# Attention of a diffusion step on one core: P left unnormalised, a fixed order in pairs, small value bands

## The chip, the cores and the metric

The kernel runs on one core of a Trainium2 chip. Its engines are TensorE (PE, with its weight loads shown apart as PEld), VectorE (DVE), ScalarE (ACT), GpSimd (POOL) and SyncE (SP, which here only issues DMAs). The metric is the device time of one execution in microseconds. Each engine runs its own instructions in order and waits at semaphores for the others.

## The reference

One step of a two-layer network: layer 0 (even) has one input projection into a recurrence branch and an attention branch and then an output projection, layer 1 (odd) is a gated recurrence. What the change touches is the attention branch of layer 0: 8 heads of 64, 1024 latent tokens on a grid of 16 rows by 64 columns, 128 context tokens.

```python
def row_block(args):                       # one grid row r, all heads
    r, q_r = args
    rs = jnp.clip(r - kh // 2, 0, rows - kh)
    k_blk = lax.dynamic_slice_in_dim(k_grid, rs, kh, axis=2)[:, :, :, col_idx]
    v_blk = lax.dynamic_slice_in_dim(v_grid, rs, kh, axis=2)[:, :, :, col_idx]
    ...
    s_loc = jnp.einsum('bhjqd,bhkjnd->bhjqkn', qb, k_blk).astype(jnp.float32) * scale + bias
    s_loc = jnp.where(valid, s_loc, NEG_INF)
    s_ctx = jnp.einsum('bhjqd,bhcd->bhjqc', qb, k_ctx).astype(jnp.float32) * scale
    s = jnp.concatenate([s_loc..., s_ctx], axis=-1)
    p = jax.nn.softmax(s, axis=-1).astype(v.dtype)
    o = (einsum(p_loc, v_blk) + einsum(p[..., n_loc:], v_ctx))
...
y = jnp.concatenate([o_a * jax.nn.silu(g_a), merge_heads(o_b) * jax.nn.silu(g_b)], axis=-1)
return y @ w_out, ...
```

Each latent query sees a window of 8 rows by 16 columns and all context keys; context queries see context keys only. The output of attention is multiplied by a SiLU gate and projected.

## The kernel before

Everything is float32 to the outside. For the projections each weight tile and each activation is split into a high part (`wh`, `hTh`) and a rest (`wl`, `hTl`), and a product is three matmuls (`mm_f`, L313 to L318). A unit (`unit_f`) is one weight tile of 128 output columns by one of three chunks of 384 tokens: 24 matmuls. A weight tile is loaded by SP (`wraw`, 512 KB), rounded by ACT (`wh`, L77) and subtracted by POOL (`wl`, L186, in `do_split`).

The order of the work is mostly that of the program: a scheduler places the instructions on each engine in advance, within the room that pools of buffers leave. "minis" are 72 tiles of [128, 384], "slabs" 20 tiles of [128, 1160]; PSUM has 3 banks of `ps_mm`, 2 of `ps_a`, 2 of `ps_b`, 1 of `ps_o`. A DMA's issue on SP waits until its target buffer is free, and what stands behind it on SP waits too.

The attention branch works on four pairs of heads, p = 0 to 3. First come the projections: for each pair three weight tiles (keys, queries, gate) of three chunks. The gate's SiLU lands in `yT` (`gate_evac`). Then come 36 items: for each pair eight grid items (half `hf` 0 or 1 of the rows, column block `j` 0 to 3; 128 queries, 384 window keys and 128 context keys, two heads `e`) and one context item. An item has three steps:

- `a_score`: for each head two matmuls into PSUM (L845 window, L848 context; queries are scaled by -1/8, so scores stand negated), the minimum of the context part (L851), one custom DVE instruction that adds the negated, masked bias and takes the minimum on (L852), the exponential on ACT with its sum (L77, `P`), the reciprocal (L856) and the scaling of P (L857).
- `a_trans`: eight 128 x 128 transposes on PE (L882) and two copies out of PSUM on ACT (`PT`, L77).
- `a_pv`: 16 value products (L897) out of the value bands, summed over keys in one bank for the four items of a half; after the fourth the gate in `yT` is multiplied by it (L905; L912 for a context item).

The loop runs transposes two items behind the scores and value products three behind, and the scheduler mixes them. The table `nbm` (mask minus bias, L822) is made by POOL for 42 of 48 tiles and by DVE for 6, each from a bias load `bT` of 192 KB. The value bands are written to DRAM and read back by column block: `band_load`, 16 loads of 256 KB into eight slabs, placed among the projections of pairs 0 to 2. Masks (`mkt`), cached context keys and values (`kc`, `vc`) and the biases of pair 0 are loaded after the first chunk of the last gate; the biases of the next pair at the end of each pair. After attention comes the out projection (L994 to L996), for which three of its eight weights are split during attention's items, the subtraction on DVE.

Of the kernel before, what the change touches and what calls it, by code (L numbers as in the profile page):

```python
# [33 lines left out]
def trunk_kernel(ctx: ExitStack, tc: tile.TileContext, x, wm0, wm, bmr, wfe, wv, woe, wfo, woo, rgw, sm, st0,  # L34
# [277 lines left out]
    def mm_f(o, i, c, k):  # L312
# [3 lines left out]
        PE.matmul(o, w1, hh, start=(k == 0), stop=False)  # L316
        PE.matmul(o, w1, hl, start=False, stop=False)  # L317
        PE.matmul(o, w2, hh, start=False, stop=(k == 7))  # L318

    def unit_f(i, c, tag=None):  # L320
# [4 lines left out]
        for k in range(8):  # L325
            mm_f(o, i, c, k)
# [479 lines left out]
    def mask_load():  # L806
        for v in range(6):
# [27 lines left out]
    def a_score(i):  # L835
        p, hf, j = items[i]
        P = slab("P", (128, 2, 512))
        nm = const.tile([128, 8], F32, name="nm", bufs=3)
        if hf >= 0:
            S = [psum("mm"), psum("o" if i % 2 else "mm")]  # L840
            for e in range(2):
                o0 = 128 + hf * 512 + j * 128
                lq = aq[p][64 * e:64 * e + 64, o0:o0 + 128]
                rk = grid(ak[p], e)[:, 4 * hf:4 * hf + 12, BS[j]:BS[j] + 32]
                PE.matmul(S[e][:, 0:384], lq, rk, start=True, stop=True)  # L845
            for e in range(2):
                o0 = 128 + hf * 512 + j * 128
                PE.matmul(S[e][:, 384:512], aq[p][64 * e:64 * e + 64, o0:o0 + 128],  # L848
                          kc_t[p][64 * e:64 * e + 64, :], start=True, stop=True)
# [523 lines left out]
```

## Time and profile before

| | |
|---|---|
| median of 3 runs | 1288.13 us (1283.86 to 1288.23) |
| profiled execution | 1288.07 us, of which the span is 1286.1 us |
| PE busy | 1207.2 us, 94% of the span |
| DVE, ACT, POOL busy | 685.7, 540.1, 381.2 us |
| projections of the attention branch end | 635.2 us after the span's start |
| attention's value products end | 777.7 us |

Busy time is what an engine's instructions cover; a busy PE may still run at half its clock, which the granted clock shows (1.00 is 2.4 GHz, 0.50 is 1.2 GHz). What follows "[" in a row of a timeline is the engine's idle time before it and what ended it. A DMA share is the mean over the core's 16 DMA engines.

### The profile page before, as it was taken

The numbers are of one execution on the slowest core, as the hardware profiler recorded it, in microseconds if no ns is written. First come the engines' busy times: TensorE is split into PE (matmuls) and PEld (weight loads), VectorE is DVE, ScalarE is ACT, GpSimd is POOL, SyncE is SP. The second block draws the span as 40 slices with busy tenths as digits, with TensorE's granted clock in tenths as the row PEclk, the third lists the DMA queues.
The fourth block names the chain that finished last, engine by engine and source line by source line (L and its number), as shares of the span: only waits on it lengthen the run. The fifth ranks groups of instructions, "written<-read, shape, count | busy, mean of one in ns | idle before, by whom it ended". The sixth has DMA issues, their size and how long they took to land.

```text
span 1286.1 us, 19174 instructions
## 1 busy us (share of the span) xinstructions
PE 1207.2 (94%) x7536; PEld 1083.1 (84%) x7536; DVE 685.7 (53%) x1422; ACT 540.1 (42%) x1065; POOL 381.2 (30%) x271
## 2 busy tenths in 40 slices
PE   4999998999999999998999999999989899988997
PEld 3889998999999997887866667888988789987886
DVE  5547128315455200000267896644678978799844
ACT  3435134324342211111246774314467576676311
POOL 0143032420515110201250420117355564644000
PEclk8999999999998999998969999999989999999999
DMA  9410100111011455523320325223001101112432
GB/s 355 186 34 21 34 17 26 40 48 37 22 35 36 156 172 189 205 87 108 128 99 17 100 83 181 81 98 131 17 26 42 42 25 42 41 33 95 137 129 82
DMA packets 41909, 110.45 MB, mean 86 GB/s; under 512 B 4180, under 2 KB 14804, under 8 KB 41820
## 3 DMA queue, kind: packets, MB, share of 16 engines
q1 hardware_dynamic: 41820, 109.24, 25.2%
q8 instruction: 59, 0.97, 0.3%
q14 instruction: 30, 0.25, 0.1%
HBM read 96.61 MB, written 12.61 MB: 85 GB/s over the span
## 4 chain that ended last, share of the span: by engine, by line
PE 52%; DVE 14%; ACT 6%; issue 4%; DMA 4%; POOL 2%; SPq 1%; POOLq 0%; ACTq 0%; DVEq 0%
PE ps_mm L316 7%; PE ps_mm L318 7%; PE ps_mm L317 7%; PE ps_mm L995 5%; PE ps_mm L996 5%; PE ps_mm L994 5%; DMA wraw<-in_wfe_dram 3%; DVE yT L1137 2%; DVE xc L1061 2%; DVE P L857 2%; ACT P L77 1%; PE ps_a L221 1%; PE ps_mm L339 1%; PE ps_mm L341 1%; PE ps_mm L340 1%
## 5 line engine op out<-in xcount | busy, mean ns | idle before, releaser
L316 PE MATMUL ps_mm<-hTh,wh 128*128 128x384 f32 x936 | 321.2, 347 | 14.6 <-ACT xp L77 4.8
L317 PE MATMUL ps_mm<-hTl,wh 128*128 128x384 f32 x936 | 320.3, 343 | 2.3 <-DVE hTl L307 1.7
L318 PE MATMUL ps_mm<-hTh,wl 128*128 128x384 f32 x936 | 319.8, 342 | 1.1 <-POOL wl L186 1.1
L186 POOL TENSOR_TENSOR wl<-wraw,wh 128x1024 fp32r<-128x1024 f32 x50 | 127.5, 2552 | 284.3 <-ACT wh L77 254.6
L316 PEld LDWEIGHTS ps_mm<-hTh,wh 128*128 128x128 f32 x936 | 178.1, 191 | 31.1 <-ACT kq L77 7.4
L317 PEld LDWEIGHTS ps_mm<-hTl,wh 128*128 128x128 f32 x936 | 178.8, 191 | 4.6 <-DVE hTl L307 3.3
L318 PEld LDWEIGHTS ps_mm<-hTh,wl 128*128 128x128 f32 x936 | 178.7, 191 | 1.9 <-POOL wl L186 1.7
L995 PE MATMUL ps_mm<-wl,yh 128*128 128x512 f32 (+1 forms) x288 | 113.6, 395 | 4.6 <-DVE wl L186 4.6
L996 PE MATMUL ps_mm<-wh,yl 128*128 128x512 f32 (+1 forms) x288 | 112.6, 391 | 0.0
L994 PE MATMUL ps_mm<-wh,yh 128*128 128x512 f32 (+1 forms) x288 | 112.4, 392 | 0.0
L77 ACT ACTIVATE wh<-wraw 128x1024 fp32r<-128x1024 f32 x68 | 71.3, 1058 | 70.5 <-DMA wraw<-in_wfe_dram 40.6
L262 POOL TENSOR_TENSOR ss<-ss,nhalf 128x1 f32<-128x1 f32 x27 | 15.2, 564 | 243.4 <-DVE ss L261 186.2
L339 PE MATMUL ps_mm<-wh,hTh 128*128 128x256 f32 x288 | 83.2, 289 | 2.1 <-ACT va L77 2.1
L341 PE MATMUL ps_mm<-wh,hTl 128*128 128x256 f32 x288 | 82.0, 285 | 0.0
L340 PE MATMUL ps_mm<-wl,hTh 128*128 128x256 f32 x288 | 81.7, 284 | 0.0
L77 ACT ACTIVATE res<-xt 128x512 f32<-128x512 f32 (+1 forms) x37 | 23.0, 621 | 123.6 <-DVE xt L1004 115.7
L995 PEld LDWEIGHTS ps_mm<-wl,yh 128*128 128x128 f32 x288 | 54.5, 189 | 19.4 <-DVE wl L186 7.7
L822 POOL TENSOR_TENSOR nbm<-mkt,bT 128x384 f32<-128x384 f32 x42 | 45.5, 1103 | 85.2 <-DVE nm L868 40.4
L365 DVE SCALAR_TENSOR_TENSOR yT<-yT,ps_mm 128x384 f32<-128x384 f32 x10 | 5.5, 554 | 113.6 <-ACT yT L77 113.6
L994 PEld LDWEIGHTS ps_mm<-wh,yh 128*128 128x128 f32 x288 | 54.4, 189 | 12.3 <-issue 0.3
L996 PEld LDWEIGHTS ps_mm<-wh,yl 128*128 128x128 f32 x288 | 54.6, 189 | 11.4
L1128 POOL TENSOR_TENSOR yT<-yT,rt 128x384 f32<-128x384 f32 x42 | 56.4, 1371 | 23.4 <-ACT rt L77 19.3
(260 smaller groups left out, 2501.1 us busy)
## 6 DMA issues: line engine op xcount, KB each, us to landing
wm<-in_wm_dram SPq DMA_DIRECT2D x48, 512.0 KB
wraw<-in_wfe_dram SPq DMA_DIRECT2D x28, 512.0 KB
xt<-in_x_dram SPq DMA_DIRECT2D x18, 512.0 KB
bT<-in_bias_dram SPq DMA_DIRECT2D x48, 192.0 KB
wraw<-in_wfo_dram SPq DMA_DIRECT2D x16, 512.0 KB
x_d<-xt SPq DMA_DIRECT2D x9, 512.0 KB
xt<-x_d SPq DMA_DIRECT2D x9, 512.0 KB
out_dram<-xt SPq DMA_DIRECT2D x18, 256.0 KB
```

What stands on the lines that cost most here:

```text
L77: i = A.activation(out, in_, func, **kw)
L186: (lo_eng or G).tensor_tensor(lo, r, hi.bitcast(F32), OP.subtract)
L316: PE.matmul(o, w1, hh, start=(k == 0), stop=False)
L317: PE.matmul(o, w1, hl, start=False, stop=False)
L318: PE.matmul(o, w2, hh, start=False, stop=(k == 7))
L339: PE.matmul(o, hh, w1, start=(k == 0), stop=False)
L340: PE.matmul(o, hh, w2, start=False, stop=False)
L341: PE.matmul(o, hl, w1, start=False, stop=(k == 7))
L994: PE.matmul(o[:, :q - p], yh[:, z], wh[:, p:q], start=(k == 0), stop=False)
L995: PE.matmul(o[:, :q - p], yh[:, z], wl[:, p:q], start=False, stop=False)
L996: PE.matmul(o[:, :q - p], yl[:, z], wh[:, p:q], start=False, stop=(k == 7))
L1128: G.tensor_tensor(us[c], us[c], r[:, c * CW:(c + 1) * CW], OP.mult)
```

## The change

1. P is left unnormalised. The sums of a pair's half, [128, 8], are doubled and inverted on DVE (`a_sums`), widened by POOL to [128, 512] (`rbw`), transposed by PE into a `ps_b` bank and multiplied into the gate (`a_gate`). L856 and L857 go. The transposed copy of the second head of every other item goes from ACT to DVE.
2. The instructions of PE and of ACT in attention are chained in program order (`ordered`), and items go in pairs: transposes, scores and value products of two items in a fixed interleaving, the gate's transposes ahead of the value products. The context item of pair 3 comes before its grid items.
3. A band is loaded for a pair of heads: 64 loads of 64 KB into six minis a pair, rather than 16 of 256 KB. The table subtraction is made in place, in the bias's buffer.
4. The projections of pair 3 go by chunk (all three weights at once), with the scores of the first two items after the last chunk's first two units. Weights of pairs 1 and 2 are loaded two ahead. Masks, caches, biases and bands of pair 0 are loaded after the chunks; the rest spread over the items. Four of the out projection's weights are split at items 11, 20, 29 and 32, on POOL.

```diff
+    def ordered(i, eng="PE"):
+
+        if eng in line:
+            after(i.ins, [line[eng]])
+        line[eng] = i.ins.name
         return i
...
-    def band_load(Rg):
-        v0 = vb_d[2 * Rg]
-        for jp in range(2):
-            t = slab("vband", (128, 2, 512))
-            vband[Rg, jp] = t
-            for jj in range(2):
-                load(t[:, jj, :], bass.AP(tensor=v0.tensor, offset=v0.offset + BS[2 * jp + jj] * 512,
-                                          ap=[[64 * 512, 4], [512, 32], [1, 512]]))
+    def band_load(p):
+
+        ts = [mini("vband") for _ in range(6)]
+        for b in range(16):
+            v0 = vb_d[2 * (b // 4)]
+            load(ts[b // 3][:, (b % 3) * 128:(b % 3 + 1) * 128],
+                 bass.AP(tensor=v0.tensor, offset=v0.offset + BS[b % 4] * 512 + p * 128,
+                         ap=[[64 * 512, 4], [512, 32], [1, 128]]))
+            vband[p, b] = ts[b // 3][:, (b % 3) * 128:(b % 3 + 1) * 128]
...
-    def bias_load(p):
-        for hf in range(2):
-            for j in range(3):
-                for h in (2 * p, 2 * p + 1):
-                    t = mini("bT")
-                    s0 = 4 if hf == 0 else 0
-                    ap = bass.AP(tensor=bias.tensor, offset=bias.offset + h * 35328 + j * 736 + s0 * 32,
-                                 ap=[[32, 8], [2208, 16], [1, 384]])
-                    load(t, ap)
-                    n = mini("nbm")
-                    (V if p == 0 and h else G).tensor_tensor(n, mkt[hf * 3 + j], t, OP.subtract)
-                    nbm[h, hf, j] = n
+    def bias_load(p, hf, j):
+        for h in (2 * p, 2 * p + 1):
+            t = mini("bT")
+            s0 = 4 if hf == 0 else 0
+            ap = bass.AP(tensor=bias.tensor, offset=bias.offset + h * 35328 + j * 736 + s0 * 32,
+                         ap=[[32, 8], [2208, 16], [1, 384]])
+            load(t, ap)
+            (V if p == 0 and h else G).tensor_tensor(t, mkt[hf * 3 + j], t, OP.subtract)
+            nbm[h, hf, j] = t
...
+    def a_sums(p, hf):
+
+        sm_ = aSum.pop((p, hf))
+        V.tensor_scalar(sm_, sm_, 2.0, None, OP.mult)
+        V.reciprocal(sm_, sm_)
+        nt = sm_.shape[1]
+        wide = slab("rbw", (128, nt * 128))
+        G.tensor_copy(wide.rearrange("p (j d) -> p j d", d=64),
+                      sm_.rearrange("p j e -> p (j e)")[:, :, None].to_broadcast([128, 2 * nt, 64]))
+        aW[p, hf] = wide
+
+    def a_gate(p, hf):
+
+        wide = aW.pop((p, hf))
+        nt = wide.shape[1] // 128
+        rb = psum("b")
+        for j in range(nt):
+            ordered(PE.transpose(rb[:, j * 128:(j + 1) * 128], wide[:, j * 128:(j + 1) * 128], ident))
+        if hf < 0:
+            yv = yT[4 + p, 0][:, 0:128]
+            V.tensor_tensor(yv, rb[:, 0:128], yv, OP.mult)
+            return
+        rb4 = rb.rearrange("p (j r c) -> p j r c", j=4, r=8)
+        for c, o0, r, n in pieces_of(hf):
+            yv = yT[4 + p, c][:, o0:o0 + n * 64].rearrange("p (r j c) -> p j r c", r=n, j=4)
+            V.tensor_tensor(yv, rb4[:, :, 8 - r % 8 - n:8 - r % 8, :][:, :, ::-1], yv, OP.mult)
...
-                act(P[:, e, :], S[e], AF.Exp, scale=-1.0, bias=nm[:, 4 * e + 1:4 * e + 2],
-                             accum_out=nm[:, 4 * e + 2:4 * e + 3])
-                V.reciprocal(nm[:, 4 * e + 3:4 * e + 4], nm[:, 4 * e + 2:4 * e + 3])
-                V.tensor_scalar(P[:, e, :], P[:, e, :], nm[:, 4 * e + 3:4 * e + 4], 0.5, OP.mult, OP.mult)
...
+    def a_exp(i):
+        p, hf, j = items[i]
+        S, nm = aS.pop(i)
+        P = slab("P", (128, 2, 512))
+        if j == 0:
+            aSum[p, hf] = const.tile([128, 4 if hf >= 0 else 1, 2], F32, name="asum" if hf >= 0 else "asumc", bufs=2)
+        n = 512 if hf >= 0 else 128
+        for e in range(2):
+            ordered(act(P[:, e, 0:n], S[e][:, 0:n], AF.Exp, scale=-1.0, bias=nm[:, 2 * e + 1:2 * e + 2],
+                        accum_out=aSum[p, hf][:, j, e:e + 1]), "ACT")
         aP[i] = P
+        if hf < 0 or j == 3:
+            a_sums(p, hf)
...
+            if e and i % 2:
+                V.tensor_copy(PT[:, e, :n * 128], pt[:, :n * 128])
+            else:
+                ordered(act(PT[:, e, :n * 128], pt[:, :n * 128], AF.Copy), "ACT")
...
-            w_get(i, 0, 1 if i + 1 < IWE else 0)
+            w_get(i, 0 if p == 0 else 2, 1)
...
+    i0 = IP + 9
+    ak[3], aq[3] = slab("kq"), slab("kq")
+    w_split(i0 + 2)
+    for c in range(3):
+        for n in range(3):
+            o = unit_f(i0 + n, c, ("a", "b", "b")[n] if c == 2 else None, ordered if c == 2 else lambda m: m)
+            proj_evac(3, n, c, o)
+            if c == 2 and n < 2:
+                a_score(n)
+                a_exp(n)
+        if c == 0:
+            mask_load(0)
+            kc_load((0,))
+            for j in range(3):
+                bias_load(0, 0, j)
+            band_load(0)
+        elif c == 1:
+            mask_load(1)
+            vc_load()
+            for j in range(3):
+                bias_load(0, 1, j)
+            kc_load((1, 2, 3))
...
     n_it = len(items)
-    for i in range(n_it + 3):
-        if 0 <= i - 2 < n_it:
-            a_trans(i - 2)
-        if i < n_it:
-            a_score(i)
-            p, hf, j = items[i]
-            if hf == 1 and j == 3 and p < 3:
-                bias_load(p + 1)
-            if hf < 0 and p >= 1:
-                w_split(IWE + p - 1, V)
-        if 0 <= i - 3 < n_it:
-            a_pv(i - 3)
+    TB = {(0, 1): (0, 0), (0, 3): (0, 1), (1, 0): (0, 2), (1, 1): (1, 0), (1, 3): (1, 1), (-1, 0): (1, 2)}
+
+    def tables(i):
+
+        p, hf, j = items[i]
+        if p < 3 and (hf, j) in TB:
+            bias_load(p + 1, *TB[hf, j])
+        if p < 3 and hf == 1 and j == 2:
+            band_load(p + 1)
+        if i in WA:
+            w_split(IWE + WA.index(i))
+
+    WA = (11, 20, 29, 32)
+    for m in range(n_it // 2 + 2):
+        ia, ib = 2 * m, 2 * m + 1
+        if 0 <= ia - 2 < n_it:
+            a_trans(ia - 2)
+        if 0 < m and ia < n_it:
+            a_score(ia)
+            a_exp(ia)
+            a_score(ib)
+        if 0 <= ib - 2 < n_it:
+            a_trans(ib - 2)
+        if 0 < m and ia < n_it:
+            a_exp(ib)
+        for i in (ia - 2, ib - 2):
+            if 0 <= i < n_it and (items[i][1] < 0 or items[i][2] == 3):
+                a_gate(*items[i][:2])
+        for i in (ia - 3, ia - 2):
+            if 0 <= i < n_it:
+                a_pv(i)
+        for i in (ia, ib):
+            if i < n_it:
+                tables(i)
     vband.clear()
 
 
```

What moves on POOL, from the last split of the projections' weights to the end of attention's tables: before, all subtractions (`nbm<-mkt,bT`) in one piece, ahead of the next layer's norm (`ss`).

```order
L186 TENSOR_TENSOR wl<-wraw,wh 128x1024
L638 TENSOR_TENSOR oss<-oss,nhalf 128x3 x2
L186 TENSOR_TENSOR wl<-wraw,wh 128x1024 x10
L822 TENSOR_TENSOR nbm<-mkt,bT 128x384 x42
L262 TENSOR_TENSOR ss<-ss,nhalf 128x1 x4
```

In the kernel after, after the same ten splits (`rbw<-asum` is the widening copy of one half of a pair, `asumc` that of a context item; the halves come in order, pair 0 first):

```order
L831 TENSOR_TENSOR bT<-mkt,bT 128x384 x14
L853 COPY rbw<-asum 128x512
L831 TENSOR_TENSOR bT<-mkt,bT 128x384 x12
L853 COPY rbw<-asum 128x512
L853 COPY rbw<-asumc 128x128
L831 TENSOR_TENSOR bT<-mkt,bT 128x384 x6
L195 TENSOR_TENSOR wl<-wraw,wh 128x1024
L831 TENSOR_TENSOR bT<-mkt,bT 128x384 x5
L853 COPY rbw<-asum 128x512
L831 TENSOR_TENSOR bT<-mkt,bT 128x384 x5
L853 COPY rbw<-asum 128x512
```

The copy of the first half of pair 0 stands behind 14 subtractions, that of its second half behind 26, that of the first half of pair 1 behind 37, that of its second half behind all 42.

SP, before, from the band loads among the projections to the biases:

```order
L56 DMA vband<-vb_d 128x1x512 x4
L56 DMA wraw<-in_wfe_dram 128x1024
L56 DMA vband<-vb_d 128x1x512 x4
L59 DMA out_dram<-kq 128x128
L56 DMA wraw<-in_wfe_dram 128x1024
L56 DMA mkt<-in_msk_dram 128x384 x6
L56 DMA kc<-in_kct_dram 128x128 x4
L56 DMA vc<-in_vcd_dram 128x256 x2
L56 DMA bT<-in_bias_dram 128x1x384 x27
L56 DMA wraw<-in_woe_dram 128x1024
L56 DMA bT<-in_bias_dram 128x1x384 x13
```

SP, after, from the loads behind the second chunk of pair 3 on (the row before these is the 16 band loads of pair 0):

```order
L56 DMA mkt<-in_msk_dram 128x384 x3
L56 DMA vc<-in_vcd_dram 128x256 x2
L56 DMA bT<-in_bias_dram 128x1x384 x6
L56 DMA kc<-in_kct_dram 128x128 x3
L56 DMA bT<-in_bias_dram 128x1x384 x8
L56 DMA vband<-vb_d 128x1x128 x16
L56 DMA bT<-in_bias_dram 128x1x384 x12
L56 DMA vband<-vb_d 128x1x128 x16
L56 DMA bT<-in_bias_dram 128x1x384 x5
L56 DMA wraw<-in_woe_dram 128x1024
L56 DMA bT<-in_bias_dram 128x1x384 x7
L56 DMA vband<-vb_d 128x1x128 x16
```

The bands now come as 16 small loads for each pair, between the biases.

PE around the gate of the second half of pair 0 in the kernel after (`P_5823` is the last item of that half, `PT_5810` and `PT_5877` its second and third, `ps_mm_5891` the context item's scores, `ps_mm_5906` the first of pair 1):

```order
L896 MATMUL ps_mm_5891<-kq_4293,kq_4384 128x128
L896 MATMUL ps_mm_5892<-kq_4293,kq_4384 128x128
L886 MATMUL ps_mm_5906<-kq_4615,kq_4729 128x384
L886 MATMUL ps_o_5907<-kq_4615,kq_4729 128x384
L888 MATMUL ps_mm_5906<-kc_5488,kq_4729 128x128
L888 MATMUL ps_o_5907<-kc_5488,kq_4729 128x128
L923 MATMUL ps_a_5917<-cs_71,P_5823 128x128 x4
L923 MATMUL ps_a_5923<-cs_71,P_5823 128x128 x4
L863 MATMUL ps_b_5933<-cs_71,rbw_5828 128x128 x4
L941 MATMUL ps_b_5840<-PT_5810,vband_5358 64x128 x2
L941 MATMUL ps_b_5840<-PT_5810,vband_5360 64x128 x2
L941 MATMUL ps_b_5840<-PT_5810,vband_5361 64x128 x2
```

PE, before, around the same context item's scores (`ps_mm_5917`):

```order
L882 MATMUL ps_a_5780<-cs_71,P_5708 128x128 x4
L897 MATMUL ps_b_5686<-PT_5734,vc_5480 64x128
L845 MATMUL ps_mm_5829<-kq_4293,kq_4384 128x384
L848 MATMUL ps_mm_5829<-kc_5472,kq_4384 128x128
L882 MATMUL ps_a_5815<-cs_71,P_5747 128x128 x4
L861 MATMUL ps_mm_5917<-kq_4293,kq_4384 128x128
L845 MATMUL ps_o_5830<-kq_4293,kq_4384 128x384
L848 MATMUL ps_o_5830<-kc_5472,kq_4384 128x128
L861 MATMUL ps_mm_5918<-kq_4293,kq_4384 128x128
L882 MATMUL ps_a_5821<-cs_71,P_5747 128x128 x4
L897 MATMUL ps_b_5893<-PT_5773,vband_5150 64x128 x2
L897 MATMUL ps_b_5893<-PT_5773,vband_5244 64x128 x2
```

Before, transposes, scores and value products are mixed as the scheduler put them. After, the transposes of the widened sums (L863) stand ahead of the value products in one fixed line.

## Rows read from the trace of the kernel before

**Rows 1.** The page: busy time, share of the span, instructions.

```profile
PE 1207.2 (94%) x7536; PEld 1083.1 (84%) x7536; DVE 685.7 (53%) x1422; ACT 540.1 (42%) x1065; POOL 381.2 (30%) x271
```

**Rows 2.** Timeline, SP’s DMA issues: start, us, line, transfer, count.

```profile
572.07 11.19 SPq L56 DMA_DIRECT2D vband<-vb_d  x4
583.35 2.57 SPq L56 DMA_DIRECT2D wraw<-in_wfe_dram  x1
```

**Rows 3.** Timeline of ACT, same stretch; in brackets its idle time before.

```profile
584.38 1.06 ACT L77 ACTIVATE wh<-wraw 128x1024 fp32r<-128x1024 f32 x1 [10.24 <-issue]
...
596.72 1.06 ACT L77 ACTIVATE wh<-wraw 128x1024 fp32r<-128x1024 f32 x1 [10.52 <-DMA wraw<-in_wfe_dram]
```

**Rows 4.** Timeline of PE around its longest idle time in the projections.

```profile
594.00 0.34 PE L317 MATMUL ps_mm<-hTl,wh 128*128 128x384 f32 x1
594.18 0.34 PE L318 MATMUL ps_mm<-hTh,wl 128*128 128x384 f32 x1
598.80 0.69 PE L316 MATMUL ps_mm<-hTh,wh 128*128 128x384 f32 x1 [4.28 <-DVE yT L365]
...
600.25 0.52 PE L317 MATMUL ps_mm<-hTl,wh 128*128 128x384 f32 x1
600.57 0.52 PE L318 MATMUL ps_mm<-hTh,wl 128*128 128x384 f32 x1
```

**Rows 5.** Windows: busy us (instructions) by engine, granted clock, DMA share, GB/s.

```profile
575.00:600.00 25.00, 18.62 (x101) 17.66 (x100) 1.57 (x3) 4.02 (x7) 5.33 (x3) 0.95 0.28 97
600.00:605.00 5.00, 5.00 (x19) 5.00 (x18) 0.00 (x0) 0.00 (x0) 0.24 (x1) 0.55 0.16 51
...
642.00:662.00 20.00, 19.85 (x74) 11.63 (x76) 11.38 (x31) 8.12 (x21) 15.54 (x15) 0.50 0.41 148
...
740.00:760.00 20.00, 18.24 (x174) 12.63 (x173) 18.14 (x60) 14.09 (x38) 9.30 (x8) 1.00 0.23 73
```

**Rows 6.** Timeline of PE: last projection matmul, first out projections, last value product.

```profile
634.99 0.34 PE L318 MATMUL ps_b<-hTh,wl 128*128 128x384 f32 x1
...
772.07 0.50 PE L994 MATMUL ps_mm<-wh,yh 128*128 128x512 f32 x1
...
777.34 0.48 PE L910 MATMUL ps_b<-PT,vbc 128*64 128x128 f32 x3
```

**Rows 7.** Timeline of PE in a packed stretch: value products, transposes, scores of one item.

```profile
692.87 0.88 PE L897 MATMUL ps_b<-PT,vband 128*64 128x128 f32 x12
...
693.89 1.09 PE L882 MATMUL ps_a<-cs,P 128*128 128x128 f32 x8
694.91 0.92 PE L845 MATMUL ps_mm<-kq 64*128 64x384 f32 x4
...
695.98 0.88 PE L897 MATMUL ps_b<-PT,vband 128*64 128x128 f32 x12
```

**Rows 8.** Groups by line and shape, 635 to 780 us: count, busy us, mean ns.

```profile
L822 POOL TENSOR_TENSOR nbm<-mkt,bT 128x384 f32<-128x384 f32 x41 | 44.5, 1105 | 72.8 <-DVE nm L868 40.4 <-DMA bT<-in_bias_dram 25.8 <-PE ps_mm L848 2.5
...
L857 DVE TENSOR_SCALAR P<-P,nm 128x512 f32<-128x512 f32 x64 | 36.5, 575 | 1.1
...
L856 DVE RECIPROCAL nm<-nm 128x1 f32<-128x1 f32 x64 | 10.1, 160 | 12.5 <-ACT P L77 12.1
...
L905 DVE TENSOR_TENSOR yT<-ps_b,yT 128x256 f32<-128x256 f32 x8 | 3.3, 410 | 0.0
```

**Rows 9.** Windows of one kind of transfer each; columns as in rows 5.

```profile
566.00:571.00 5.00, 5.00 (x31) 5.00 (x30) 0.00 (x0) 0.00 (x0) 0.00 (x0) 1.00 0.26 103
...
625.00:627.00 2.00, 2.00 (x13) 2.00 (x12) 0.00 (x0) 0.00 (x0) 0.00 (x0) 1.00 0.96 286
627.00:628.50 1.50, 1.50 (x11) 1.50 (x10) 0.56 (x1) 0.49 (x1) 0.00 (x0) 1.00 0.45 140
...
710.00:722.00 12.00, 11.50 (x98) 7.80 (x96) 11.37 (x33) 7.38 (x20) 11.45 (x11) 1.00 0.54 172
```

**Rows 10.** Timeline of SP: the first bias issues.

```profile
629.04 3.43 SPq L56 DMA_DIRECT2D bT<-in_bias_dram  x5
```

**Rows 11.** Timeline of POOL: its first subtraction.

```profile
632.92 1.02 POOL L822 TENSOR_TENSOR nbm<-mkt,bT 128x384 f32<-128x384 f32 x1 [12.44 <-DMA bT<-in_bias_dram]
```

More of the change, by code (lines that the diff above doesn't have):

```diff
@@ L80, in act @@
             chain["users"].append(i.ins.name)
+        return i
+    line = {}
+    def ordered(i, eng="PE"):
+        if eng in line:
+            after(i.ins, [line[eng]])
+        line[eng] = i.ins.name
         return i
@@ L315, in mm_f, with unit_f @@
         w1, w2 = wh[:, k * 128:(k + 1) * 128], wl[:, k * 128:(k + 1) * 128]
[L316 to L320, printed above, removed]
+        keep(PE.matmul(o, w1, hh, start=(k == 0), stop=False))
+        keep(PE.matmul(o, w1, hl, start=False, stop=False))
+        keep(PE.matmul(o, w2, hh, start=False, stop=(k == 7)))
+    def unit_f(i, c, tag=None, keep=lambda m: m):
         ucount[0] += 1
@@ L794, in trunk_kernel, with kc_load @@
     nbm = {}
-    def cache_load():
-        for p in range(4):
+    def kc_load(ps):
+        for p in ps:
             t = mini("kc")[:, 0:128]
@@ L800, in cache_load, with vc_load @@
             kc_t.append(t)
+    def vc_load():
         for b in range(2):
@@ L804, in cache_load, with mask_load @@
             vc_t.append(t)
-    def mask_load():
-        for v in range(6):
+    def mask_load(hf):
+        for v in range(3 * hf, 3 * hf + 3):
             t = mini("mkt")
@@ L825, in trunk_kernel, with pieces_of @@
     items = []
     for p in range(4):
-        items += [(p, hf, j) for hf in range(2) for j in range(4)]
-        items.append((p, -1, 0))
+        grid_items = [(p, hf, j) for hf in range(2) for j in range(4)]
+        items += [(p, -1, 0)] + grid_items if p == 3 else grid_items + [(p, -1, 0)]
     JT = (0, 1, 1, 2)
-    aR, aP, aPT, aO = {}, {}, {}, {}
+    aP, aPT, aO, aSum, aW, aS = {}, {}, {}, {}, {}, {}
+    def pieces_of(hf):
+        for c in range(3):
+            for o0, r, n in rows_of(c):
+                if r // 8 == hf:
+                    yield c, o0, r, n
@@ L844, in a_score @@
                 rk = grid(ak[p], e)[:, 4 * hf:4 * hf + 12, BS[j]:BS[j] + 32]
[L845 removed]
+                ordered(PE.matmul(S[e][:, 0:384], lq, rk, start=True, stop=True))
             for e in range(2):
[L847 to L849 removed]
+                ordered(PE.matmul(S[e][:, 384:512], aq[p][64 * e:64 * e + 64, o0:o0 + 128],
+                                  kc_t[p][64 * e:64 * e + 64, :], start=True, stop=True))
@@ L856, in a_score @@
-                V.reciprocal(nm[:, 4 * e + 3:4 * e + 4], nm[:, 4 * e + 2:4 * e + 3])
-                V.tensor_scalar(P[:, e, :], P[:, e, :], nm[:, 4 * e + 3:4 * e + 4], 0.5, OP.mult, OP.mult)
+                                       nm[:, 2 * e:2 * e + 1], OP.add, OP.min, nm[:, 2 * e + 1:2 * e + 2])
         else:
-            S = [psum("mm"), psum("o" if i % 2 else "mm")]
             for e in range(2):
-                PE.matmul(S[e][:, 0:128], aq[p][64 * e:64 * e + 64, 0:128],
-                          ak[p][64 * e:64 * e + 64, 0:128], start=True, stop=True)
+                ordered(PE.matmul(S[e][:, 0:128], aq[p][64 * e:64 * e + 64, 0:128],
+                                  ak[p][64 * e:64 * e + 64, 0:128], start=True, stop=True))
@@ L909, in a_pv @@
                 cc = slice((2 * p + e) * 64, (2 * p + e) * 64 + 64)
-                PE.matmul(o[64 * e:64 * e + 64, 0:128], vbc[:, cc], PT[:, e, 0:128], start=True, stop=True,
-                          skip_group_check=True)
+                ordered(PE.matmul(o[64 * e:64 * e + 64, 0:128], vbc[:, cc], PT[:, e, 0:128], start=True, stop=True,
+                          skip_group_check=True))
             V.tensor_tensor(yT[4 + p, 0][:, 0:128], o[:, 0:128], yT[4 + p, 0][:, 0:128], OP.mult)
```

80 lines of the change are left out of this document (32 added, 48 removed).

## The prediction

> **What bounds the kernel now.** Read the page first: TensorE (PE) is busy for 94% of the span of 1286.1 us [rows 1], so a gain is an idle PE, a half clock, or PE work that goes. Then read the windows of the two stages that the change touches.
>
> The end of the projections. In 575 to 600 us PE is busy for 18.62 us of 25 and idle for 6.4 [rows 5]; the longest piece is 4.28 us before 598.80 [rows 4]. ACT is in order, and its `wh` cast stands there with 10.2 and 10.5 us of idle time before it [rows 3], the projections' evacuations queued behind. The weights come late because SP issues them late: four value-band loads wait for slabs over 11.19 us ahead of the weight issued at 583.35 [rows 2]. After the idle time the matmul pitch is 0.32 us (600.25 to 600.57) against 0.18 (594.00 to 594.18), up to 604.4, with a granted clock of 0.55 in 600 to 605 [rows 4, 5]: the 1.2 GHz level. That is 17 matmuls x 0.15 = 2.5 us lost.
>
> Attention runs from 635.2 (last projection matmul) to 777.7 (last value product) [rows 6]; 15 out-projection matmuls of 0.23 us lie inside (3.5 us, the first at 772.07), so it takes 139.0 us. A packed item needs 1.02 us of value products, 1.02 of transposes and 1.07 of scores, 3.11 in all [rows 7]; 32 grid items would take 99.5 us. The other 39 us: 642 to 662 runs at a clock of 0.50, where 20 us do 10 us of work, and in 740 to 760 DVE is busy for 18.14 of 20 us [rows 5] and holds PE.
>
> **The change part by part.**
>
> Weights two ahead, and no slabs for bands: the four band loads leave SP's queue there. I take the whole idle time and the half clock as gone: -6.4 - 2.5 = -8.9 us (bounds 0 and -8.9: nothing later in the projections waits as long). The first two items' scores move between the last units: two x 1.07 = +2.1 us there, taken from attention.
>
> DVE. 64 scalings (575 ns) and 64 reciprocals (160 ns) go: 36.5 + 10.1 = 46.6 us [rows 8]. Eight sums of [128,8] are doubled and inverted (16 instructions, some 0.16 us each, 2.6), the gate is multiplied once more in the shapes of L905/L912 (410 ns for the middle one [rows 8], 20 pieces, 8 us), and about 16 PT copies come over from ACT (0.6 us, 10 us). Net -26 us over 36 items, 0.7 an item: DVE falls from what 740 to 760 shows to under 3 us an item, beneath PE's 3.11.
>
> PE. 36 transposes for the gate, each an eighth of 1.02 us: +4.6. With everything ready attention would be 99.5 + 3.8 (four context items at 0.95) + 4.6 - 2.1, and some 8 for its start, its end and gates that wait for a ps_b buffer: 114 us, 25 less than now. That is the kernel if no wait takes the place of the old ones.
>
> The DMAs and POOL. This is where I think it goes wrong. POOL is in order, and the change puts the gate's widening copy (L853) into the same queue as the bias subtractions (L831), each of which waits for its DMA. In the order of POOL, 26 subtractions stand before the copy of the second half of pair 0, and 42, all of them, before that of the second half of pair 1. In the order of PE the gate's transposes wait for that copy, and since PE is now fixed, all that follows waits too. In the kernel before nothing but the subtractions was in this queue: its 25.8 us of waiting for bT [rows 8] delayed nobody for as long.
>
> What must land before these copies: masks and caches (6 + 4 + 2 loads, 1.70 MB), 32 or 48 biases, 32 or 64 band loads.
> - Masks and caches at 286 GB/s [rows 9]: 6 us.
> - A bias (192 KB) at 172 GB/s: 1.14 us. The share is 0.54 of 16 engines, so about 8 work [rows 9].
> - A band load: in 566 to 571 only 256 KB band loads run, at 103 GB/s and a share of 0.26, so about 4 engines, 2.55 us each [rows 9]. The new one has the same outer dimension of 4, a quarter of the bytes, in pieces of 512 B instead of 2 KB. Lower bound by bytes: 0.64 us. For 512 B pieces the cache loads at 627 are the nearest row: 140 GB/s at a share of 0.45, 19.4 GB/s an engine, 26 ns a piece; 32 pieces on one engine make 0.84 us. I take 0.84. A pair's bands cost 13.5 us, and the three pairs that were loaded under the projections before are now loaded in attention.
>
> I take the streams as adding, bands and biases on the same engines: the weight issued at 583.35 behind four bands was cast 13.4 us later [rows 2, 3], so what is issued behind bands waits for them. The Trainium skill, "DMA: Bandwidth & Descriptors", section "Why a DMA increments its semaphore by 16 and not by 1", says that a DMA from SP takes the largest number of engines up to 16 that divides both sides' slowest dimension, and the lowest-numbered ones: 4 for a band and 8 for a bias, with the 4 among the 8. The shares 0.26 and 0.54 agree with the numbers; no row shows which engines they are. By that rule the streams queue; without its second half they could run side by side (the first rival).
>
> Clock from t = 0, the end of the last projection unit. The stream starts when the first chunk of pair 3 gives its buffers free: seven units before (7 x 24 x 0.174 = 29.2) and the two scores (2.1), t = -31; first data at -29.
> - Up to the last bias before the first copy in question: 6 + 32 x 1.14 + 32 x 0.84 = 69.4, t = +40. From issue to start of the subtraction a lone bias took 3.9 us (629.04 to 632.92 [rows 10, 11]), so about 2 after the data; subtraction 1.1 [rows 8], copy about 1 (taken like a subtraction): t = +44. PE wants it after 8 items of transposes, 8 of scores and 5 of value products, t = +24 to +26. Stall about 18 us.
> - The first out-projection weight is issued behind two more pairs' bands and five biases; its cast stands in ACT's queue, which the change fixes too, ahead of PT copies: some 9 us more.
> - Up to the last biases: 6 + 48 x 1.14 + 64 x 0.84 + 1.8 (the weight) = 116, t = +87, with 2 us of gaps where SP waits for a buffer. The last two biases are issued only when the subtraction of an earlier one has given its buffer free: another 3 + 3.9 + 2.2. Copy: t = +98. PE would be there at +85.
> - Behind that copy stand 18 value products, 16 transposes, 14 scores and the gates: 18 x 1.02 + 16 x 1.02 + 14 x 1.07 + 1.7 (context) + 3 = 54.4, and some 9 for waits on ps_b, the end and the clock: it falls after such a stall, by 2.5 us as at 598.80 or by 10 as in 642 to 662; I take 4. End: t = +161.
>
> Before it was 139.0. So +161 + 2.1 - 139.0 - 8.9 = +15 us. The profiled run took 1288.07 us (1.97 beside the span), the median is 1288.13, so: **1303 us**. The early scores, the clock lost at 642 and DVE's relief give nothing in this case, since they lie before the last copy, whose time the DMAs set.
>
> **The rivals.**
> - *The streams don't add, or the queue is let through sooner:* bands and biases on different engines. Then 48 x 1.14 + 6 stands against 114 us of PE work, no stall is over a few us, and attention takes 114 to 128 us: 1288 - 8.9 + 2.1 - (11 to 25) = 1256 to 1270. For it: PE-bound work is short by a quarter, and no row shows the shared engines. Against it: a band moves at 0.26 of the engines, and a wraw behind such loads at 583.35 was cast 13 us later [rows 2, 3]: the queue does hold what is behind.
> - *Small pieces cost only their bytes:* 0.64 us, 64 x 0.2 = 13 us less: about 1290, no change. The Trainium skill, same page, section "Specifications", gives 512 B as enough for line rate and some 27 GiB/s an engine: 0.56 us by that as an estimate, and about 1285. The 19.4 GB/s an engine of the cache loads is less; the row decides.
> - *The forecast's own mechanism, slower:* POOL's copy behind the DMAs, decisive from the point where the stream's end plus 63 us passes 145 (t = +82): 1296 to 1312, at the long half clock up to 1313.
> - *The change doesn't do what it says in the projections:* the new prefetch waits for slabs just so, the 8.9 us stay: 1312.
>
> **How the numbers follow.** A measurement of this kernel tells 0.5% (6.4 us) from no change. The slower case 0.52, with 0.04 for the projections unchanged: slower 0.56. Cheap small pieces, or half of the stall hidden: 0.10 within 0.5%. No shared queue: 0.34 faster. The slower case alone spans 1296 to 1313. The range for 8 in 10 must reach into the fast case: 1262 to 1313, with some 0.13 below and 0.07 above.
>
> **What would show it.** POOL's waits in the new profile: L831 on DMA bT or vband's queue for some 40 us in attention, and L853 late. PE idle before L863, released by POOL, twice 10 us or more, at about 44 and 98 us after the last projection unit. A DMA share of 0.25 to 0.54 without a break up to +87. In the projections no idle over 1 us at the band loads' old place. DVE under 15 of 20 us in the last pairs. The forecast is wrong if the band loads of a pair take under 8 us, if DMA share passes 0.7 while bands and biases run together, or if PE waits for the gate less than 5 us in all.

## The result, and the profile after

The kernel after takes 1295.92 us (median of 5 runs, 1291.66 to 1300.75) where the kernel before took 1288.13: a ratio of 1.0093, with an interval of 1.0063 to 1.0122. It is slower by more than 0.5%.

The profiled execution has a span of 1291.7 us against 1286.1. Busy time, to be read beside [rows 1]:

```profile
PE 1183.7 (92%) x7572; PEld 1078.3 (83%) x7572; DVE 658.2 (51%) x1336; ACT 529.9 (41%) x1047; POOL 391.8 (30%) x287
```

PE is busy for 23.5 us less in a span that is 5.6 us longer, so 29 us more of it is idle. (Busy time is not work: PE has 36 matmuls more than before.) The next rows tell where the span changed: PE's last projection matmul and its last value product in the kernel after.

```profile
623.32 0.34 PE L327 MATMUL ps_b<-hTh,wl 128*128 128x384 f32 x1
...
782.27 0.39 PE L941 MATMUL ps_b<-PT,vc 128*64 128x128 f32 x4
```

Against [rows 6] the projections end 11.7 us earlier (623.7 for 635.3) and attention takes 159.0 us for 139.0. The rest, counted as in the prediction, takes 509.0 for 511.8. So -11.7 + 20.0 - 2.8 = +5.5 us. Of the 11.7, 3.4 were there before the change acts: the same matmul, in the stage before, stands at 388.39 here and at 391.79 before.

PE in attention, the idle times of over 3.5 us:

```profile
664.39 0.90 PE L863 MATMUL ps_b<-cs,rbw 128*128 128x128 f32 x3 [12.96 <-POOL rbw L853]
...
686.20 1.11 PE L923 MATMUL ps_a<-cs,P 128*128 128x128 f32 x4 [7.62 <-ACT PT L77]
...
718.96 1.11 PE L863 MATMUL ps_b<-cs,rbw 128*128 128x128 f32 x4 [12.10 <-POOL rbw L853]
723.93 0.45 PE L863 MATMUL ps_b<-cs,rbw 128*128 128x128 f32 x1 [3.85 <-DVE yT L871]
```

They make 36.5 us. The first and the third stand before the gate's transposes and name the widening copy on POOL. Look at POOL there:

```profile
650.86 3.08 POOL L831 TENSOR_TENSOR bT<-mkt,bT 128x384 f32<-128x384 f32 x3 [13.29 <-DMA bT<-in_bias_dram]
654.56 9.22 POOL L831 TENSOR_TENSOR bT<-mkt,bT 128x384 f32<-128x384 f32 x9 [0.62 <-DMA bT<-in_bias_dram]
663.73 0.61 POOL L853 COPY rbw<-asum 128x512 f32<-128x512 f32 x1
...
709.84 1.94 POOL L831 TENSOR_TENSOR bT<-mkt,bT 128x384 f32<-128x384 f32 x2 [14.48 <-DMA bT<-in_bias_dram]
715.82 0.99 POOL L831 TENSOR_TENSOR bT<-mkt,bT 128x384 f32<-128x384 f32 x1 [4.04 <-DMA bT<-in_bias_dram]
717.36 0.99 POOL L831 TENSOR_TENSOR bT<-mkt,bT 128x384 f32<-128x384 f32 x1 [0.55 <-DMA bT<-in_bias_dram]
718.30 0.61 POOL L853 COPY rbw<-asum 128x512 f32<-128x512 f32 x1
```

The copy takes 0.61 us; what makes it late is the row of subtractions ahead of it, and what makes those late is the biases' DMAs. The biases are late because SP issues them behind the bands (SP's issues; the second column is how long it took to get them out, which includes what SP waits for meanwhile):

```profile
629.24 16.02 SPq L56 DMA_DIRECT2D vband<-vb_d  x16
645.36 9.73 SPq L56 DMA_DIRECT2D bT<-in_bias_dram  x12
655.53 16.14 SPq L56 DMA_DIRECT2D vband<-vb_d  x16
671.76 3.47 SPq L56 DMA_DIRECT2D bT<-in_bias_dram  x5
675.28 0.44 SPq L56 DMA_DIRECT2D wraw<-in_woe_dram  x1
```

The weight at 675.28 is the cause of the idle time before 686.20: ACT's cast of it stands ahead of the copies that PE waits for. After SP, POOL and ACT a fourth queue, DVE's, has the same trouble. DVE's first split of the out projection's activations (`yl`) waits for POOL's last subtraction. It reads nothing of that subtraction, so it must be its buffer that it waits for: by the program's order that of a mask (`mkt`), which the last subtraction reads; the trace names the subtraction alone. ACT and DVE of the kernel after:

```profile
684.61 1.06 ACT L77 ACTIVATE wh<-wraw 128x1024 fp32r<-128x1024 f32 x1 [8.96 <-DMA wraw<-in_woe_dram]
```

```profile
718.39 1.59 DVE L1061 TENSOR_TENSOR yl<-yT,yh 128x384 fp32r<-128x384 f32 x2 [13.88 <-POOL bT L831]
```

Windows of the same stretch (columns as in [rows 5]) show the price beside the idle time, which is the lower granted clock:

```profile
640.00:650.00 10.00, 10.00 (x115) 8.12 (x115) 7.51 (x27) 7.93 (x21) 0.00 (x0) 1.00 0.37 99
650.00:664.00 14.00, 1.42 (x14) 1.05 (x10) 2.48 (x10) 2.80 (x9) 12.11 (x13) 0.62 0.48 161
664.00:680.00 16.00, 13.23 (x107) 9.97 (x107) 7.78 (x28) 3.76 (x11) 2.56 (x4) 0.80 0.48 123
...
700.00:719.00 19.00, 6.43 (x69) 4.98 (x67) 4.26 (x15) 4.84 (x14) 4.57 (x6) 0.80 0.34 96
719.00:740.00 21.00, 17.14 (x157) 13.62 (x157) 15.60 (x54) 13.48 (x35) 3.75 (x3) 0.77 0.00 1
...
760.00:780.00 20.00, 19.58 (x202) 15.59 (x203) 14.64 (x51) 15.65 (x38) 3.82 (x4) 1.00 0.31 101
```

In the last pairs DVE is busy for 14.64 of 20 us, where it was 18.14 [rows 5], and PE is packed: the relief is there, but only after the last of the late loads.

### The profile page after: what moved, and what is told of

Same layout as the page of the kernel before. It is cut to its first block, busy times and chain, and to the rows that moved or that the text cites. A ratio compares the mean times of both kernels' runs of the same rounds, so it can differ in the third digit from the quotient of the medians.

```text
span 1291.7 us, 19168 instructions
## 1 busy us (share of the span) xinstructions
PE 1183.7 (92%) x7572; PEld 1078.3 (83%) x7572; DVE 658.2 (51%) x1336; ACT 529.9 (41%) x1047; POOL 391.8 (30%) x287
## 4 chain that ended last, share of the span: by engine, by line
PE 58%; DVE 12%; ACT 4%; issue 4%; DMA 3%; POOL 2%; SPq 0%; POOLq 0%; ACTq 0%; DVEq 0%
PE ps_mm L325 8%; PE ps_mm L326 8%; PE ps_mm L327 8%; PE ps_mm L1079 4%; PE ps_mm L1080 4%; PE ps_mm L1078 4%; DVE yT L1221 3%; PE ps_b L941 2%; PE ps_a L923 2%; DVE xc L1145 2%; DMA bT<-in_bias_dram 2%; PE ps_mm L886 1%; PE ps_a L230 1%; PE ps_mm L348 1%; PE ps_mm L350 1%
## 5 line engine op out<-in xcount | busy, mean ns | idle before, releaser
L325 PE MATMUL ps_mm<-hTh,wh 128*128 128x384 f32 x928 | 315.5, 344 | 8.8 <-ACT xp L77 4.8
L326 PE MATMUL ps_mm<-hTl,wh 128*128 128x384 f32 x928 | 315.3, 340 | 2.3 <-DVE hTl L316 1.7
L327 PE MATMUL ps_mm<-hTh,wl 128*128 128x384 f32 x928 | 314.5, 339 | 0.4 <-POOL wl L195 0.4
L195 POOL TENSOR_TENSOR wl<-wraw,wh 128x1024 fp32r<-128x1024 f32 x54 | 136.8, 2538 | 253.4 <-ACT wh L77 213.9
L325 PEld LDWEIGHTS ps_mm<-hTh,wh 128*128 128x128 f32 x928 | 174.9, 189 | 24.3 <-issue 5.6
L326 PEld LDWEIGHTS ps_mm<-hTl,wh 128*128 128x128 f32 x928 | 175.6, 189 | 4.7 <-DVE hTl L316 3.3
L327 PEld LDWEIGHTS ps_mm<-hTh,wl 128*128 128x128 f32 x928 | 175.3, 189 | 1.0 <-POOL wl L195 0.8
L271 POOL TENSOR_TENSOR ss<-ss,nhalf 128x1 f32<-128x1 f32 x27 | 15.2, 564 | 220.6 <-DVE ss L270 164.7
L831 POOL TENSOR_TENSOR bT<-mkt,bT 128x384 f32<-128x384 f32 x42 | 41.6, 998 | 99.5 <-DMA bT<-in_bias_dram 95.2
L348 PEld LDWEIGHTS ps_mm<-wh,hTh 128*128 128x128 f32 x288 | 54.2, 188 | 2.8 <-ACT va L77 2.8
```

The costliest lines, as they stand in the source:

```text
L195: (lo_eng or G).tensor_tensor(lo, r, hi.bitcast(F32), OP.subtract)
L325: keep(PE.matmul(o, w1, hh, start=(k == 0), stop=False))
L326: keep(PE.matmul(o, w1, hl, start=False, stop=False))
L327: keep(PE.matmul(o, w2, hh, start=False, stop=(k == 7)))
L348: PE.matmul(o, hh, w1, start=(k == 0), stop=False)
```

## The experiments

Theory at the start: one row of loads, issued by SP, is too long for the pairs, and POOL's copy behind it stops PE. Each edit is against the kernel after. Ratios are to the kernel before, timed on the same chip; the kernel after stands at 1.0093. Diffs show the lines that matter.

**copy_dve**: the widening copy off POOL's queue.

```diff
-        G.tensor_copy(wide.rearrange("p (j d) -> p j d", d=64),
+        V.tensor_copy(wide.rearrange("p (j d) -> p j d", d=64),
```

> One edit to the kernel after: the widening copy (L853) runs on DVE, behind the inversion of its sums, rather than in POOL's queue behind the bias subtractions. Theory (POOL's queue): PE's two waits before L863, 13.0 and 12.1 us, go; the stream of loads is as it was, so ACT's cast of the first out-projection weight, queued at item 11, still waits for a weight that lands some 60 us after the last projection unit, and PE stands for about 20 us there instead of 7.6. End of attention 139 us after the last projection unit instead of 159: 1275 us (1268 to 1284). Rival (the fixed order in pairs itself costs the time, whatever the copy waits for): 1290 to 1296. Rival (the bands' time on the DMA engines sets everything, the queue only passes it on): over 1290, PE then waits at DVE's bias subtraction results.

1301.78 us, 1.0102 (1.0035 to 1.017): a miss, no faster than the kernel after. PE no longer waits for POOL, but:

```profile
685.41 1.97 PE L923 MATMUL ps_a<-cs,P 128*128 128x128 f32 x8 [24.01 <-ACT PT L77]
...
724.45 0.45 PE L863 MATMUL ps_b<-cs,rbw 128*128 128x128 f32 x1 [17.73 <-DVE yT L871]
```

ACT's cast and DVE's split behind these two:

```profile
683.81 1.06 ACT L77 ACTIVATE wh<-wraw 128x1024 fp32r<-128x1024 f32 x1 [25.36 <-DMA wraw<-in_woe_dram]
```

```profile
718.81 0.56 DVE L1061 TENSOR_TENSOR yl<-yT,yh 128x384 fp32r<-128x384 f32 x1 [14.79 <-POOL bT L831]
```

PE reached the other two queues sooner and waited there for the same loads. The copy alone is not what counts.

**bands16**: band loads with an outer count of 32 instead of 4; the exponential writes P with its keys in the matching order, and the cached values are loaded so.

```diff
-                         ap=[[64 * 512, 4], [512, 32], [1, 128]]))
+                         ap=[[512, 32], [64 * 512, 4], [1, 128]]))
...
```

> One edit to the kernel after: keys within a block of 4 rows by 32 columns are ordered column first, so that the band loads have an outer dimension of 32 rather than 4 (same bytes, same 512 B pieces, same number of loads; the exponential writes P in the new order, the context values are loaded in it). The copy stays on POOL. Theory (a band takes 4 engines for 0.9 us, and these carry the biases too): DMA share in a stretch of bands alone rises from 0.30 towards 0.5 or more, a band costs what its issue costs on SP, about 0.55 us, the three pairs' bands 17 us less; the copy of pair 1's second half comes at about 75 us after the last projection unit instead of 95, PE waits under 12 us before L863 in all: 1274 us (1266 to 1284). Rival (SP's issue and its eight loads under way set the pace, not the engines): no band faster than 0.9 us, 1292 to 1297. Rival (bands and biases on different engines): under 5 us of gain.

1286.72 us, 1.0023 (0.9984 to 1.0061): a miss, in the right direction with less than half of the size. Sixteen bands still take SP over 13 us; the bytes (64 KB) and the pieces (512 B) are the same as before.

```profile
627.61 13.09 SPq L56 DMA_DIRECT2D vband<-vb_d  x16
...
650.34 13.20 SPq L56 DMA_DIRECT2D vband<-vb_d  x16
```

These rows hold more than the bands' own pace: SP begins them while the biases before them still move. Where bands alone move, the rate tells it (last two columns: share of the 16 DMA engines, GB/s). The kernel after, then bands16:

```profile
663.00:672.00 9.00, 7.61 (x55) 5.80 (x55) 1.53 (x5) 0.49 (x2) 1.57 (x3) 0.58 0.29 76
```

```profile
686.00:694.00 8.00, 8.00 (x98) 6.80 (x96) 6.37 (x23) 6.93 (x14) 1.72 (x3) 1.00 0.36 103
```

A band of 64 KB is 0.86 us at 76 GB/s and 0.64 us at 103 (0.70 in 658 to 663 us of bands16, at 93). (The packets of the two windows average 500 and 470 B: a band's pieces of 512 B and little else; a bias's have 1536.)

**both** (the two edits together) and **both_w** (besides, the later output weights due later):

```diff
-    WA = (11, 20, 29, 32)
+    WA = (20, 26, 29, 32)
```

> Both edits at once: copy on DVE and bands with an outer dimension of 32. Theory: no wait before L863; the first out-projection weight lands at about 48 us instead of 61, PE stands some 9 us behind ACT's cast at item 11; 1264 us (1257 to 1272). If POOL's queue alone were at fault this would be no better than the copy alone, if the loads alone, no better than the bands alone.

> As the run before, and the out-projection weights are split at items 20, 26, 29 and 32 rather than 11, 20, 29 and 32, so that no weight is waited for behind the loads of pairs 2 and 3. Theory: no stall over 3 us left in attention, PE-bound at 3.1 us an item, 114 to 122 us for attention: 1256 us (1250 to 1263). Rival (fixed order in pairs costs by itself): attention over 128 us, 1265 or more.

1289.85 us, 1.0031 (0.9999 to 1.0064), and 1291.41 us, 1.0041 (1.0011 to 1.007): both missed, and neither is faster than bands16 alone. In the first PE waits 15.22 us for ACT at 677.63 and 11.66 us for DVE at 710.90. In the second one queue is left, and it takes all; DVE of both_w:

```profile
715.62 0.56 DVE L1065 TENSOR_TENSOR yl<-yT,yh 128x384 fp32r<-128x384 f32 x1 [24.55 <-POOL bT L831]
```

PE's idle time there, at 721.26, is 27.69 us.

**clear**: the copy on DVE, the later weights, and no band loads for the second to fourth pair (the first pair's are used again).

> The changed kernel without the 48 band loads of the second to fourth pair (the first pair's bands are used again, so the values of those pairs are other ones), with the gate's copies on DVE instead of POOL, and the later output weights due at items 20 and 26 instead of 11 and 20. Theory (the row of loads sets the time, and the fixed order in pairs costs nothing by itself): no idle time of PE over 4 us in the pairs, the pairs as short as 120 to 126 us where the changed kernel has 159, 1256 us (1250 to 1263). Rival (the order in pairs costs itself, by DVE and ACT waits): the idle times shrink, but PE waits in many small pieces, and 1270 us or more.

1277.44 us, 0.9936 (0.9912 to 0.9961): a miss, 14 us above the range. PE has one long wait, 17.62 us at 675.96, for ACT, which stands at the first cast of the split, again for POOL's last subtraction:

```profile
675.21 0.52 ACT L77 ACTIVATE yh<-yT 128x384 fp32r<-128x384 f32 x1 [18.32 <-POOL bT L831]
```

So even without 48 of the loads the split's place in the queue costs. The rival's many small pieces did not come: beside this no idle time is over 3.3 us.

**bias16**: the partitions of a bias in the order (column, row), so that its load has an outer count of 16 instead of 8; queries, gate and masks are permuted to match.

```diff
-                         ap=[[32, 8], [2208, 16], [1, 384]])
+                         ap=[[2208, 16], [32, 8], [1, 384]])
...
```

> The changed kernel with the partitions of a window's bias in the order (column, row) instead of (row, column), so that the outer count of each bias load is 16 instead of 8; bytes and pieces stay. Theory (the load's time on its engines sets the row's pace): a bias costs 0.25 to 0.38 us less, the copy for the second pair's second half comes 12 to 16 us earlier, 1282 us (1276 to 1288). Rival (SP's time to issue a load sets the pace): the copies stay where they were within 4 us, 1292 us or more.

1279.04 us, 0.993 (0.989 to 0.997), inside what the theory gave. The copy for the second pair's second half is at 703.36 instead of 718.30, 15 us earlier, where 12 to 16 were expected. What became cheaper is the bias, as the theory had it. Two windows in which biases move, the kernel after and then bias16:

```profile
651.00:659.00 8.00, 0.42 (x4) 0.19 (x2) 2.25 (x8) 2.04 (x5) 7.15 (x8) 0.65 0.53 185
```

```profile
623.50:628.00 4.50, 4.50 (x32) 3.44 (x30) 3.15 (x9) 2.44 (x7) 3.69 (x5) 1.00 0.96 282
```

A bias of 192 KB is 1.06 us at 185 GB/s and 0.70 us at 282. SP's rows alone would tell it wrongly:

```profile
626.21 13.27 SPq L56 DMA_DIRECT2D vband<-vb_d  x16
639.57 9.74 SPq L56 DMA_DIRECT2D bT<-in_bias_dram  x12
649.40 12.25 SPq L56 DMA_DIRECT2D vband<-vb_d  x16
```

The bands, which were not touched, go out in 13.27 and 12.25 us instead of 16.02 and 16.14, and the twelve biases need as long as before. But the bands' own rate has not changed, 76 GB/s as in the kernel after:

```profile
655.00:662.00 7.00, 4.09 (x33) 3.76 (x35) 0.76 (x2) 0.00 (x0) 3.09 (x5) 0.50 0.29 76
```

SP runs ahead of the data, and the loads under way hold it back. In the kernel after it begins the second row of bands at 655.53, inside the first window above, in which the engines still move biases; so that row's 16.14 us hold the end of the biases. PE still waits for POOL's copy in bias16, 11.13 us at 657.91 and 10.79 at 704.03: the row is shorter, the queue is as it was.

**free**: the chain of `ordered` off.

> The changed kernel without the chain that fixes the order of PE, ACT and DVE in the attention: the scheduler orders them, with the loads and their order on SP and POOL as they were. Theory (the row of loads sets the time): the two waits for POOL's copy stay at their places, 1290 to 1300 us. Rival (the fixed order itself costs): 1275 us or less.

1294.9 us, 1.0066 (1.0029 to 1.0103). PE waits 14.57 us (at 669.00) and 10.74 us (at 723.29) for POOL's copy. The stops stay without the fixed order, so it does not make them.

**queues**: no load changed; the copy on DVE, the later weights, and the splits held until the exponentials of item 25 are through.

```diff
...
-            act(hi, yv, AF.Copy)
-            V.tensor_tensor(lo, yv, hi.bitcast(F32), OP.subtract)
+            after(act(hi, yv, AF.Copy).ins, [line["YA"]])
+            after(V.tensor_tensor(lo, yv, hi.bitcast(F32), OP.subtract).ins, [line["YV"]])
```

> The changed kernel with all its loads as they are (bands with an outer count of 4, biases of 8), but with the three in-order queues cleared: the gate's copies on DVE, the later output weights due at items 20 and 26, the first splits of the output projection's activations held until item 25 is through. Theory A (the queues turn a late load into a stop of PE; the row of loads itself is in time for the scores and the masks): no idle time of PE over 4 us in the pairs, 1268 us (1262 to 1274). Theory B (the row itself is too long, whatever stands behind it): the waits move on to the masks of the third and fourth pair, 1278 us or more.

1281.76 us, 0.9977 (0.9945 to 1.0008). Theory B has the size, but not the place: masks and scores are in time. PE runs to 693 without an idle time of over 3 us, and then waits once, 24.13 us, for ACT, which waits for the first output weight at the end of the row:

```profile
711.04 0.33 SPq L56 DMA_DIRECT2D wraw<-in_woe_dram  x1
```

```profile
716.28 1.06 ACT L77 ACTIVATE wh<-wraw 128x1024 fp32r<-128x1024 f32 x1 [24.50 <-DMA wraw<-in_woe_dram]
```

**best2** and **best2_again** (one kernel, timed twice): bands16, bias16 and queues together.

> The changed kernel with five edits: band loads with an outer count of 32, bias loads with an outer count of 16, the gate's copies on DVE, the later output weights due at items 20 and 26, and the first splits of the output projection's activations held on ACT and DVE until item 25 is through, so that DVE does not stand at a tile that a mask still holds. Theory (three in-order queues hold PE behind one row of loads: POOL's copy, ACT's cast, DVE's split; all three are now clear of it): no idle time of PE over 4 us in the pairs, 1257 us (1250 to 1264). Rival (a fourth queue stands behind the same row, or the row itself is too long for the scores): one idle time of 10 us or more stays, 1275 to 1290.

> The kernel best2 once more, timed in more rounds beside the three above on one chip: 1264 us (1260 to 1268), ratio to the kernel before 0.980 to 0.987; PE has no idle time over 4 us in the pairs.

1264.13 us, 0.9829 (0.975 to 0.9909), and 1263.31 us, 0.9816 (0.9776 to 0.9856): the first at the upper end of its range, 7 us above its middle, the second as expected, and both faster than both kernels. In the second run's trace:

```profile
625.81 11.87 SPq L56 DMA_DIRECT2D vband<-vb_d  x16
637.77 7.65 SPq L56 DMA_DIRECT2D bT<-in_bias_dram  x12
645.51 10.51 SPq L56 DMA_DIRECT2D vband<-vb_d  x16
...
687.29 0.47 SPq L56 DMA_DIRECT2D wraw<-in_woe_dram  x1
```

The same weight is issued at 687.29 instead of 711.04 in queues. ACT does not wait for it, and no idle time of PE in the pairs is over 2.5 us. The pairs take 124.8 us (626.9 to 751.7).

**best2_free**: best2 without the chain.

> The kernel best2 without the chain that fixes the order on PE, ACT and DVE in the attention. Theory (with the loads out of the way the order of both is nearly the same, and the loads were what counted): 1264 us, within 5. Rival (the fixed order in pairs is what makes best2 fast): 1272 us or more.

1261.59 us, 0.9796 (0.9751 to 0.9841): the same as best2. The gain is not the fixed order's.

**no_prefetch**: the weights of pairs 1 and 2 with no lead.

```diff
-            w_get(i, 0 if p == 0 else 2, 1)
+            w_get(i, 0, 1)
```

> The changed kernel with the weights of the second and third pair's projections loaded with no lead, in a call of w_get(i, 0, 1). Theory (the lead took away the ACT casts' waits of 10 us, and with them PE's idle time and its half clock in the last projections): the last projection ends 6 to 10 us later than in the changed kernel, PE idle times of 2 us or more come back between 560 and 600 us, and the whole is 1300 to 1306 us. Rival (the early scores alone fill the projections): the last projection ends within 2 us of where it did, 1292 to 1297 us.

1299.12 us, 1.0097 (1.006 to 1.0134): a miss, with the ratio of the kernel after. Its last projection is late by the span, but not by its stage (PE, the reference point of the stage before and the end):

```profile
398.99 0.53 PE L571 MATMUL ps_a<-eb,kp 128*128 128x64 f32 x2 [2.15 <-ACT at L77]
...
634.70 0.34 PE L327 MATMUL ps_b<-hTh,wl 128*128 128x384 f32 x1
```

The 10.6 us at 399 come from a stretch that the edit does not touch (granted clock 0.70 in 200 to 240 us, 0.96 in the kernel after). From there to the end it is 235.7 us, 234.9 in the kernel after and 243.2 before. Between 560 and 623 us PE has no idle time. So the lead was worth 0.8 of 8.3 us.

## Why the prediction was right, point by point

The forecast (slower, by POOL's copy behind the loads) held; 1303 us was 7 us too much, and 1295.92 lies just below the foot of the case's own range, 1296 to 1313.

- **The mechanism, its places and its times held.** Copies through at t = +44 and +98 predicted, at +40.7 and +95.3 in the trace (t = 0 at 623.7). PE's stops: 18, 9 and 13 us predicted; 12.96, 7.62 and 12.10 + 3.85 found. From the last copy to the last value product 63 us predicted, 63.7 found. Attention +22 predicted, +20.0 found.
- **The terms of the row held, where one kind of load moves alone.** A band at 0.84 us: 76 GB/s, so 0.86. A bias at 1.14: 185 GB/s, so 1.06. A pair's row was 27.1 us by the prediction and is 26.3 on SP, from its first band to the next pair's (629.24 to 655.53). The row began at t = -35.0 (the first mask, 588.61), four us sooner than predicted; from there to the two copies it took 75.7 and 130.3 us, for 75 and 129 predicted. The rival that small pieces cost only their bytes (0.64) falls with the 0.86.
- **"I take the streams as adding" held:** biases and bands take turns, at a share of 0.53 in 651 to 659 us and of 0.29 in 663 to 672. Which engines carry which load no run shows. By the Trainium skill, "DMA: Bandwidth & Descriptors", section "Why a DMA increments its semaphore by 16 and not by 1", an outer count of 32 gives a band 16 engines where 4 gave it 4, so each would carry a quarter of the pieces; the trace has 0.64 to 0.70 us for 0.86, and by that rule alone one would have looked for more. With a share of 0.36 in that window the engines are not what holds these bands: SP takes 10.25 us to issue the sixteen of that row (from 683.35), the same 0.64 each.
- **The projections: right size, wrong edit.** -8.9 predicted, -8.3 - 2.1 = -10.4 found (without the 3.4 that were there before). But the two-ahead lead, named first in that step, gave 0.8; no_prefetch takes it away. What is left is the second half of that step, that bands no longer stand in SP's row among these weights: before, SP issues bands from 552 on between them [rows 2], after, the first at 597.35, behind all of them. That this is the cause is argued from the order of the row; no run put the bands back, or undid the new order of pair 3's projections alone.
- **Not foreseen:** the fourth queue (the split on ACT and DVE that waits for the last subtraction), which the prediction never names. In the kernel after it cost little, because POOL's copy stopped PE first: the idle time that names DVE is 3.85 us, and 2.48 of that are there in best2_again too, where the splits are held back; both_w shows it at 27.69. And the out projection, 2.8 us shorter; that the weights split earlier do this was not tested.
- **Where the 7 us are:** the sum was +15.2. Attention took 2.0 less than that, the projections with their early scores 1.5, the out projection 2.8: +8.9, against +7.8 by the medians. (The profiled execution has 3.4 less, from its first 390 us, which the change does not touch.)
- **The rival "the streams don't add" had the right sum for a kernel without the waits:** 114 to 128 us of attention, 1256 to 1270. best2_again has 124.8 and 1263.31. Its reason was another: not that loads run side by side, but that the row becomes short and no in-order queue stands behind its end.

What stays open: whether queues with still later weights, without the edits to the loads, would do as well as best2; whether the two edits to the loads alone would (no run has both without the queues' edits); and why SP takes 0.64 us to issue a band.

## What to carry to other kernels

When a wait is found, list every in-order queue that stands behind the same late transfer before taking one out of it: here POOL's copy, ACT's cast and a split on ACT and DVE held PE in turn, and removing one or two left the time as it was; with all of them clear attention fell from 159.0 to 142.5 us (queues), with the row shorter alone to 143.3 (bias16), and with both to 124.8. The buffer that a later stage will take from the pool is such a wait too, though no line of the code shows it. And a load's cost is read from a window in which it moves alone, not from how long the issuing queue took over it: that time holds the loads before it too.

## What the runs showed of the hardware

- The time that SP takes to issue a row of loads is not the loads' own: the same sixteen bands were issued in 16.14 us behind biases of outer count 8 and in 12.25 behind biases of 16, and moved at 76 GB/s and 0.29 of the engines in both.
- The outer count of a load changed its rate, with bytes and pieces as they were: 8 to 16 took a bias from 185 to 282 GB/s (0.53 to 0.96 of the engines), 4 to 32 a band from 76 to between 93 and 103 GB/s (0.29 to between 0.32 and 0.36).
- An idle time of 13 us leaves a half clock (0.50, 1.2 GHz) behind: PE resumes at 664.39 in the kernel after, and the granted clock of the window around it is 0.50:

```profile
658.00:670.00 12.00, 5.61 (x40) 4.62 (x42) 0.76 (x2) 0.44 (x2) 6.38 (x8) 0.50 0.35 102
```

  In best2_again, without such stops, the three windows from 623 to 740 us have 0.95, 0.96 and 1.00.
